# Raw query and key weights in tiles of their own, and a fixed order of two engines in the last two products

## The chip, the cores and the metric

The kernel runs on one core of a Trainium2 chip. The metric is the device time of one execution in microseconds (us), the median of several runs. The core has five engines with a queue each: PE (TensorE, matmuls; its weight loads are shown apart as PEld), DVE (VectorE), ACT (ScalarE), POOL (GpSimd) and SP (SyncE), which here issues nearly all DMAs. Each engine takes its own queue in order; semaphores tie them together.

## The reference, cut to what matters

One layer of an encoder for 1024 frames of 1024 channels, in float32:

```
h = x + W_out( GroupRMSNorm( concat[ attention(n), conv(n), gating(n) ] ) ),   n = RMSNorm(x) * g
y = RMSNorm( h + W_down( relu( W_up RMSNorm(h) )^2 ) ) * g_final

attention: 8 heads of 64; queries of a chunk of 64 frames see their own chunk and the 8 before it,
           scores * 64**-0.5 + bias by clipped distance, softmax, times values
```

The query, key and value columns are part of one input projection `w_in` (512 columns each). The last step is an RMSNorm: each row of 1024 is divided by the root of its mean square and multiplied by a gain.

## The kernel before, in words

All products are made in a split form: a float32 operand is written as a rounded part `hi` (ACT, a copy, L52) and a remainder `lo` (DVE, a subtraction, L53), and one product is three matmuls (`mm3`, L64 to L66). So each weight that comes in raw by DMA costs one ACT and one DVE instruction (`split`) before PE can use it.

**Attention.** Heads go in four pairs p = 0 to 3. For each pair the key weights (a raw tile of 128 x 1024) and the query weights are loaded (`Proj.load`, L344), split into the slots `wh` and `wl` of pool `W` (two each), and multiplied with the normed input in two halves of 512 frames (`Proj.steps`); `evac` (L388) copies each half from PSUM into the projected rows `kc` or `qc`. `expand` (L398 to L403) then makes from `kc` and `qc` the operands of each of the two heads: `kh`, `kl` and `q`, with two copies by DMA (L399, L401). The raw weights and the projected rows have one and the same tile: `raw` takes a tile of tag `QC` (two slots, one for keys and one for queries), the load writes the weights into it, the split reads them, and the evacuation writes the rows over them. So the raw key weights of pair p + 1 need the slot in which the projected keys of pair p lie, until the last `expand` of pair p has read it.

The 64 units of attention (pair, head, tile of 128 frames) run in a loop: `softmax` of the next unit, `turn` (transposes of the probabilities to `pt` on PE, split into `pth` on ACT, L510, and `ptl` on DVE, L511), `values` (L537) and `scores`. Between them `fill_to` feeds PE with steps of the projections of the later pairs and of the other two branches, in the order of `stream`: keys and queries of pair 1, `cg` 0, keys and queries of pair 2, `xh` 0, keys and queries of pair 3, and so on. `expand` for the first head of pair p + 1 stands at unit 12 of pair p, for the second at unit 15. `stream` splits the next weights in the middle of a projection and issues the load of the ones after.

**The order of the work.** Outside of blocks of `manual_schedule` a planner orders each engine's queue: by the order of the program, but with an estimate of when operands and slots are there, so an instruction that it holds ready goes ahead of one that waits. In a block of `manual_schedule` the engines that are named take their instructions in the order of the program.

**The end.** The down projection is seven products per block of the inner dimension (`PLAN`), four blocks. The last two products of the last block (m = 3 and m = 4) each finish four tiles of 128 rows, one PSUM bank after another: bank u of 4 takes 12 matmuls, then `add` puts it on the accumulator `acc` (DVE, L876). `finish` follows: `square` of the half that was just added (ACT, L1166, with the sum over the row), the sum of both halves scaled (DVE, L1176), the power -1/2 (POOL, L1178), the two halves scaled into `o` (DVE, L1184; for the last tile one half on ACT, L1182) and two writes (SP, L1185). The tile `o` has two buffers.

Of the kernel before, what the change touches and what calls it, by code (L numbers as in the profile page):

```python
# [30 lines left out]
def trunk(ctx, tc, x, mix_g, w_in, rb_rev, conv_w, sg_ln_g, sg_ln_b, sg_w, sg_b,  # L31
# [13 lines left out]
    def big(tag, shape, dt, name):  # L45
        return L.tile(shape, dt, tag=tag, bufs=SLOTS[tag], name=name)
# [52 lines left out]
    def half(hf):  # L99
        return slice(hf * HALF, (hf + 1) * HALF)  # L100
# [280 lines left out]
    def qk_projs(p):  # L381
        def one(nm, c0, sc):
            def raw():
                qkc[nm, p] = big("QC", [P, T], F32, f"{nm}c{p}")
                return qkc[nm, p].rearrange("p (k m) -> p k m", k=NK)

            def evac(hf, ps):
                A.activation(qkc[nm, p][:, hf * HALF:(hf + 1) * HALF], ps, AF.Copy, scale=sc)  # L388
            return Proj(c0 + p * P, f"{nm}{p}", evac, raw)
        return [(o, hf) for o in (one("k", 512, 1.0), one("q", 0, 0.125)) for hf in range(2)]  # L390
# [484 lines left out]
    def add(out, a, b):  # L875
        V.tensor_tensor(out, a, b, op=ALU.add)  # L876
# [291 lines left out]
    def early_half(t, k):  # L1168
        square(t, k)
        V.tensor_scalar(sums[t][:, 2:3], sums[t][:, k:k + 1], 1.0 / D, EPS, op0=ALU.mult, op1=ALU.add)  # L1170

    def finish(t, k):

        ss = sums.get(t)
        square(t, k)
        V.scalar_tensor_tensor(ss[:, 3:4], ss[:, k:k + 1], 1.0 / D, ss[:, 2:3], op0=ALU.mult, op1=ALU.add)  # L1176
        r = sm.tile([P, 1], F32, tag="rf", name="rf")
        G.tensor_tensor(r, ss[:, 3:4], mhalf[:, 0:1], op=ALU.pow)  # L1178
        o = E_.tile([P, D], F32, tag="o", bufs=2, name=f"o{t}")
        for i in (k, 1 - k):  # L1180
            if t + 1 == NT and i != k:
                A.activation(o[:, half(i)], acc[t][:, half(i)], AF.Copy, scale=r)  # L1182
            else:
                V.scalar_tensor_tensor(o[:, half(i)], acc[t][:, half(i)], r, gfin[:, half(i)], op0=ALU.mult, op1=ALU.mult)  # L1184
            load(out[t * P:(t + 1) * P, half(i)], o[:, half(i)])  # L1185
# [11 lines left out]
        ready[n] = [down_ops(PLAN[s][0], p) for p in BLOCKS[b]]  # L1197

    load_down(BLOCKS[0], (1,))
    banks = {}  # L1200
    for n, (b, s) in enumerate(steps):
        if n + 1 < len(steps):
            prep(n + 1)
        if n == 0:
            open_acc(0, 0)
            load_down(BLOCKS[0], (0,))
        elif n in (2, 3, 5):
            open_acc(*{2: (0, 1), 3: (1, 1), 5: (1, 0)}[n])
        elif n == 14:
            load(gfin, fin_g.partition_broadcast(P))  # L1210
        m, which, start, (i, k) = PLAN[s]
        ops = ready.pop(n)
        last = b == len(BLOCKS) - 1
        for u in range(4):
            sl = slice(u * P, (u + 1) * P)
            if start:
                banks[which, u] = bank(f"d{which}{u}")
            ps = banks[which, u]
            for j, (ho, wo_) in enumerate(ops):
                mm3(ps, ho[:, 0, sl], ho[:, 1, sl], wo_[:, 0], wo_[:, 1], start and j == 0, j == len(ops) - 1,  # L1220
                    skip_group_check=True)
            t = 4 * i + u
            add(acc[t][:, half(k)], ps, acc[t][:, half(k)])
            if last and m in (2, 7):
                early_half(t, k)
            if last and m == 7 and t + 1 == NT:
                V.tensor_tensor(acc[t][:, half(k)], acc[t][:, half(k)], gfin[:, half(k)], op=ALU.mult)
            if last and m in (3, 4):
                finish(t, k)


_INS = ["x", "mix_norm_g", "w_in", "rel_bias", "conv_w", "sg_ln_g", "sg_ln_b", "sg_w", "sg_b",
# [24 lines left out]
```

## Time and profile before

| | |
|---|---|
| median of 3 runs | 1120.9 us (1120.43 to 1121.08) |
| the profiled execution, its own time | 1118.65 us |
| span of the profiled execution (first to last instruction) | 1116.9 us |
| PE busy | 1090.4 us (98%) |
| weight loads busy | 911.8 us (82%) |
| DVE, ACT, POOL busy | 746.9 (67%), 551.5 (49%), 73.2 us (7%) |

The page of the profile gives busy times for one execution; the span is shorter than the execution's own time by what lies before the first and after the last instruction. In the page's slices of 28 us PE is busy at nine tenths or more in all but the first and the last. Views of the trace used below: the waits (who waited for whom, in total us, times, and the longest), the timeline (start, duration, engine, line, operation, and in brackets the idle time before it with what ended it), the instructions of one tile, windows (busy us of each engine in a stretch) and the DMA issues.

### The profile page before, as it was taken

What the parts mean: (1) busy time and instruction counts of PE and PEld (TensorE: products, weight loads), DVE (VectorE), ACT (ScalarE), POOL (GpSimd) and SP (SyncE); (2) the same over time, 40 slices, a digit from 0 to 9 for tenths busy, and PEclk for the clock granted to TensorE, in tenths of its full rate; (3) what the DMA queues carried; (4) which work ended last, traced back from release to release, by engine and by line L of the source; (5) the groups of instructions that cost most, each with busy time, mean ns of one, the idle gap of its engine ahead of it and who ended that gap; (6) DMA issues with size and microseconds to landing.
All of it is one profiled execution on the core that took longest, in us unless ns stands there. A gap on an engine that the chain in (4) does not pass through costs nothing.

```text
span 1116.9 us, 14983 instructions
## 1 busy us (share of the span) xinstructions
PE 1090.4 (98%) x5377; PEld 911.8 (82%) x5377; DVE 746.9 (67%) x1430; ACT 551.5 (49%) x1094; POOL 73.2 (7%) x131
## 2 busy tenths in 40 slices
PE   7999999999999999999999999999999999999996
PEld 6889987887888788887888888888878888888884
DVE  5526477667676761569766656564499978869775
ACT  5434376555664630467555555555544433434442
POOL 1101023101021210000000000000000000000001
PEclk8999999999999999999999999999999999999998
DMA  7523013021120143452543535353698545263303
GB/s 244 184 68 80 1 24 88 18 53 47 43 58 23 39 151 131 151 208 104 177 172 122 189 115 196 113 189 125 250 340 280 196 165 188 86 207 103 96 20 150
DMA packets 83197, 145.16 MB, mean 130 GB/s; under 512 B 6050, under 2 KB 41652, under 8 KB 83124
## 3 DMA queue, kind: packets, MB, share of 16 engines
q1 hardware_dynamic: 82548, 142.38, 37.8%
q10 hardware_dynamic: 576, 1.84, 0.4%
q8 instruction: 42, 0.69, 0.3%
q14 instruction: 31, 0.25, 0.1%
HBM read 98.58 MB, written 41.42 MB: 125 GB/s over the span
## 4 chain that ended last, share of the span: by engine, by line
PE 85%; DVE 7%; DMA 4%; ACT 2%; issue 1%; POOL 0%; SPq 0%; POOLq 0%; DVEq 0%; ACTq 0%
PE uA L66 5%; PE uA L65 5%; PE uA L64 5%; PE dA L66 5%; PE dA L64 5%; PE dA L65 4%; PE dB L64 3%; PE dB L66 3%; PE dB L65 3%; PE av L537 3%; PE uC L64 2%; PE uC L66 2%; PE uC L65 2%; PE o L64 2%; PE o L65 2%; PE o L66 2%
## 5 line engine op out<-in xcount | busy, mean ns | idle before, releaser
L52 ACT ACTIVATE ho<-hr 128x512 fp32r<-128x512 f32 x112 | 69.0, 623 | 140.7 <-PE dA L66 51.2
L64 PE MATMUL dA<-wo,ho 128*128 128x512 f32 x256 | 99.7, 390 | 0.8 <-ACT ho L52 0.8
L66 PE MATMUL dA<-wo,ho 128*128 128x512 f32 x256 | 99.3, 390 | 0.5 <-DVE ho L53 0.5
L65 PE MATMUL dA<-wo,ho 128*128 128x512 f32 x256 | 99.5, 389 | 0.0
L53 DVE TENSOR_TENSOR ho<-hr,ho 128x512 fp32r<-128x512 f32 x112 | 76.8, 690 | 15.7 <-ACT ho L52 15.7
L64 PE MATMUL dB<-wo,ho 128*128 128x512 f32 x192 | 74.8, 390 | 0.0
L66 PE MATMUL dB<-wo,ho 128*128 128x512 f32 x192 | 74.8, 390 | 0.0
L65 PE MATMUL dB<-wo,ho 128*128 128x512 f32 x192 | 74.7, 389 | 0.0
L53 DVE TENSOR_TENSOR wo<-wd,wo 128x512 fp32r<-128x512 f32 x96 | 65.6, 689 | 2.3 <-ACT wo L52 2.3
L52 ACT ACTIVATE wo<-wd 128x512 fp32r<-128x512 f32 x96 | 58.8, 619 | 10.1 <-DVE wd L879 6.2
L485 ACT ACTIVATE pr<-s,st 128x640 f32<-128x640 f32 (+2 forms) x64 | 42.3, 661 | 36.9 <-DVE st L480 26.6
L64 PEld LDWEIGHTS dA<-wo,ho 128*128 128x128 f32 x256 | 48.0, 188 | 11.3 <-ACT ho L52 1.5
L66 PEld LDWEIGHTS dA<-wo,ho 128*128 128x128 f32 x256 | 48.0, 188 | 11.1 <-DVE ho L53 1.1
L65 PEld LDWEIGHTS dA<-wo,ho 128*128 128x128 f32 x256 | 48.1, 188 | 9.9
L510 ACT ACTIVATE pth<-pt 128x512 fp32r<-128x512 f32 (+2 forms) x96 | 40.0, 435 | 32.1 <-PE pt L506 31.4
L876 DVE TENSOR_TENSOR acc<-dA,acc 128x512 f32<-128x512 f32 x64 | 43.8, 690 | 16.7 <-PE dA L66 15.0
L511 DVE TENSOR_TENSOR ptl<-pt,pth 128x512 fp32r<-128x512 f32 (+2 forms) x96 | 45.2, 487 | 12.9 <-ACT pth L510 11.9
L64 PE MATMUL o<-woh,mxh 128*128 128x512 f32 x128 | 50.6, 399 | 0.0
L66 PE MATMUL o<-woh,mxl 128*128 128x512 f32 x128 | 50.0, 391 | 0.0
L65 PE MATMUL o<-wol,mxh 128*128 128x512 f32 x128 | 50.0, 390 | 0.0
L1178 POOL TENSOR_TENSOR rf<-ssf,mhalf 128x1 f32<-128x1 f32 x8 | 4.4, 551 | 617.4 <-DVE ssf L1176 617.4
L876 DVE TENSOR_TENSOR hid<-uC,v 128x512 f32<-128x512 f32 x15 | 10.4, 691 | 51.5 <-PE uC L66 51.5
(344 smaller groups left out, 3083.0 us busy)
## 6 DMA issues: line engine op xcount, KB each, us to landing
wr_u<-in_w_up SPq DMA_DIRECT2D x32, 512.0 KB, 4.3
wd<-in_w_down SPq DMA_DIRECT2D x32, 512.0 KB, 4.6
wr_o<-in_w_out SPq DMA_DIRECT2D x8, 512.0 KB, 4.3
xr<-in_x SPq DMA_DIRECT2D x8, 512.0 KB, 4.9
hs<-h SPq DMA_DIRECT2D x8, 512.0 KB, 3.7
acc<-hs SPq DMA_DIRECT2D x16, 256.0 KB, 6.5
out_y<-o SPq DMA_DIRECT2D x16, 256.0 KB, 2.1
x<-in_x SPq DMA_DIRECT2D x7, 512.0 KB, 3.9
```

The costliest lines, as they stand in the source:

```text
L52: A.activation(hi, raw, AF.Copy)
L53: V.tensor_tensor(lo, raw, hi.bitcast(F32), op=ALU.subtract)
L64: PE.matmul(ps, lhsT=sh, rhs=mh, start=start, stop=False, **kw)
L65: PE.matmul(ps, lhsT=sh, rhs=ml, start=False, stop=False, **kw)
L66: PE.matmul(ps, lhsT=sl, rhs=mh, start=False, stop=stop, **kw)
L485: A.activation(pr[:, :b - a], s[:, a:b], AF.Exp, bias=st[:, 2:3], accum_out=lsum[p, t // 4][:, lc:lc + 1])
L510: A.activation(dh, src, AF.Copy)
L511: V.tensor_tensor(dl, src, dh.bitcast(F32), op=ALU.subtract)
L537: PE.matmul(dst, lhsT=lhs, rhs=rhs, start=first, stop=(i == len(kbs) - 1 and ph == 1))
L876: V.tensor_tensor(out, a, b, op=ALU.add)
L1178: G.tensor_tensor(r, ss[:, 3:4], mhalf[:, 0:1], op=ALU.pow)
```

## The change

First, the raw weights of keys and queries get a tag of their own, `kw`, in the pool of the attention stage, with two slots; the tile of tag `QC` is taken at the first evacuation, for the projected rows alone. Second, from the last product but one on, ACT and DVE are in a block of `manual_schedule`, and `finish` is taken apart: `square` follows the add of its tile at once, `rate` (sum and power) comes ahead of the next tile's add, and the scalings and writes of a tile come after the add and the square of the next.

```diff
--- before.py
+++ after.py
@@ -381,10 +381,11 @@
     def qk_projs(p):
         def one(nm, c0, sc):
             def raw():
-                qkc[nm, p] = big("QC", [P, T], F32, f"{nm}c{p}")
-                return qkc[nm, p].rearrange("p (k m) -> p k m", k=NK)
+                return AP_.tile([P, NK, P], F32, tag="kw", bufs=2, name=f"wr_{nm}{p}")
 
             def evac(hf, ps):
+                if hf == 0:
+                    qkc[nm, p] = big("QC", [P, T], F32, f"{nm}c{p}")
                 A.activation(qkc[nm, p][:, hf * HALF:(hf + 1) * HALF], ps, AF.Copy, scale=sc)
             return Proj(c0 + p * P, f"{nm}{p}", evac, raw)
         return [(o, hf) for o in (one("k", 512, 1.0), one("q", 0, 0.125)) for hf in range(2)]
@@ -1169,13 +1170,15 @@
         square(t, k)
         V.tensor_scalar(sums[t][:, 2:3], sums[t][:, k:k + 1], 1.0 / D, EPS, op0=ALU.mult, op1=ALU.add)
 
+    def rate(t, k):
+
+        ss = sums[t]
+        V.scalar_tensor_tensor(ss[:, 3:4], ss[:, k:k + 1], 1.0 / D, ss[:, 2:3], op0=ALU.mult, op1=ALU.add)
+        rates[t] = sm.tile([P, 1], F32, tag="rf", name="rf")
+        G.tensor_tensor(rates[t], ss[:, 3:4], mhalf[:, 0:1], op=ALU.pow)
+
     def finish(t, k):
-
-        ss = sums.get(t)
-        square(t, k)
-        V.scalar_tensor_tensor(ss[:, 3:4], ss[:, k:k + 1], 1.0 / D, ss[:, 2:3], op0=ALU.mult, op1=ALU.add)
-        r = sm.tile([P, 1], F32, tag="rf", name="rf")
-        G.tensor_tensor(r, ss[:, 3:4], mhalf[:, 0:1], op=ALU.pow)
+        r = rates[t]
         o = E_.tile([P, D], F32, tag="o", bufs=2, name=f"o{t}")
         for i in (k, 1 - k):
             if t + 1 == NT and i != k:
@@ -1197,7 +1200,7 @@
         ready[n] = [down_ops(PLAN[s][0], p) for p in BLOCKS[b]]
 
     load_down(BLOCKS[0], (1,))
-    banks = {}
+    banks, whole, rates, man = {}, [], {}, ExitStack()
     for n, (b, s) in enumerate(steps):
         if n + 1 < len(steps):
             prep(n + 1)
@@ -1211,6 +1214,8 @@
         m, which, start, (i, k) = PLAN[s]
         ops = ready.pop(n)
         last = b == len(BLOCKS) - 1
+        if n + 2 == len(steps):
+            man.enter_context(tc.manual_schedule(engines={mybir.EngineType.Activation, mybir.EngineType.DVE}))
         for u in range(4):
             sl = slice(u * P, (u + 1) * P)
             if start:
@@ -1220,13 +1225,21 @@
                 mm3(ps, ho[:, 0, sl], ho[:, 1, sl], wo_[:, 0], wo_[:, 1], start and j == 0, j == len(ops) - 1,
                     skip_group_check=True)
             t = 4 * i + u
+            if whole:
+                rate(*whole[0])
             add(acc[t][:, half(k)], ps, acc[t][:, half(k)])
             if last and m in (2, 7):
                 early_half(t, k)
             if last and m == 7 and t + 1 == NT:
                 V.tensor_tensor(acc[t][:, half(k)], acc[t][:, half(k)], gfin[:, half(k)], op=ALU.mult)
             if last and m in (3, 4):
-                finish(t, k)
+                square(t, k)
+                whole.append((t, k))
+                if len(whole) > 1:
+                    finish(*whole.pop(0))
+    rate(*whole[0])
+    finish(*whole.pop())
+    man.close()
 
 
 _INS = ["x", "mix_norm_g", "w_in", "rel_bias", "conv_w", "sg_ln_g", "sg_ln_b", "sg_w", "sg_b",
```

## Rows read from the trace of the kernel before

**Rows 1.** The page, its first line.
```profile
span 1116.9 us, 14983 instructions
```

**Rows 2.** Waits of PE, then of its weight loads: total us, times, longest.
```profile
PE pt L506 <- DVE ptl L511: 3.7, 2, 1.9
...
PEld pt L506 <- DVE ptl L511: 4.5, 2, 2.3
```

**Rows 3.** Timeline around 190 us: start, us, engine, line, operation [idle before, releaser].
```profile
185.04 1.22 DVE L400 TENSOR_TENSOR kl<-kc,kh 64x1024 fp32r<-64x1024 f32 x1
186.29 0.39 SPq L344 DMA_DIRECT2D kc<-in_w_in  x1
...
192.22 1.06 ACT L52 ACTIVATE wh_k<-kc 128x1024 fp32r<-128x1024 f32 x1 [1.91 <-DMA kc<-in_w_in]
192.34 0.34 PE L466 MATMUL s<-kh,q 128*128 128x384 f32 x1
192.52 0.33 PE L467 MATMUL s<-kl,q 128*128 128x384 f32 x1
...
193.32 1.22 DVE L53 TENSOR_TENSOR wl_k<-kc,wh_k 128x1024 fp32r<-128x1024 f32 x1 [2.22 <-ACT wh_k L52]
194.46 0.28 DVE L511 TENSOR_TENSOR ptl<-pt,pth 128x128 fp32r<-128x128 f32 x1
194.80 0.33 PE L506 MATMUL pt<-ident,pr 128*128 128x128 f32 x1 [1.94 <-DVE ptl L511]
```

**Rows 4.** Timeline around 250 us.
```profile
256.18 0.40 PE L65 MATMUL xh<-nl,wh_xh 128*128 128x512 f32 x1
...
258.37 0.33 PE L506 MATMUL pt<-ident,pr 128*128 128x128 f32 x1 [1.80 <-DVE ptl L511]
```

**Rows 5.** Timeline of PE, its last 48 matmuls, first and last.
```profile
1095.07 0.39 PE L64 MATMUL dA<-wo,ho 128*128 128x512 f32 x1
...
1105.72 0.39 PE L66 MATMUL dA<-wo,ho 128*128 128x512 f32 x1
```

**Rows 6.** Timeline of DVE at the end, from the last add but one.
```profile
1107.83 0.68 DVE L876 TENSOR_TENSOR acc<-dA,acc 128x512 f32<-128x512 f32 x1
1109.37 0.16 DVE L1176 SCALAR_TENSOR_TENSOR ssf<-ssf 128x1 f32<-128x1 f32 x1 [0.85 <-ACT sq L1166]
1109.44 0.69 DVE L876 TENSOR_TENSOR acc<-dA,acc 128x512 f32<-128x512 f32 x1
1110.19 1.42 DVE L1184 SCALAR_TENSOR_TENSOR o<-acc,rf,gfin 128x512 f32<-128x512 f32 x2
1111.52 0.15 DVE L1176 SCALAR_TENSOR_TENSOR ssf<-ssf 128x1 f32<-128x1 f32 x1
1112.34 0.75 DVE L1184 SCALAR_TENSOR_TENSOR o<-acc,rf,gfin 128x512 f32<-128x512 f32 x1 [0.66 <-POOL rf L1178]
```

**Rows 7.** Timelines of SP (97 to 158 us) and ACT (175 us).
```profile
97.23 0.56 SPq L344 DMA_DIRECT2D qc<-in_w_in  x1
157.94 0.47 SPq L399 DMA_DIRECT2D kh<-kh  x1
...
175.74 0.60 ACT L388 ACTIVATE qc<-q 128x512 f32<-128x512 f32 x1 [0.57 <-PE q L66]
```

**Rows 8.** Tiles `xn` and `xT`: durations, first and last start.
```profile
L91 DVE SCALAR_TENSOR_TENSOR xn<-x,rs,gmix x7: 1277/1284/1285, 16.0 to 35.8; 128x1024 f32<-128x1024 f32 x7
...
L218 PE MATMUL xT<-ident,xn x64: 270/273/476, 9.9 to 54.5; 128*128 128x128 f32 x64
```

**Rows 9.** Timelines of ACT and POOL at the end.
```profile
1108.61 0.63 ACT L1166 ACTIVATE sq<-acc 128x512 f32<-128x512 f32 x1 [2.97 <-DVE acc L876]
...
1109.61 0.55 POOL L1178 TENSOR_TENSOR rf<-ssf,mhalf 128x1 f32<-128x1 f32 x1 [3.14 <-DVE ssf L1176]
```

**Rows 10.** DMA issues of the output: size, us to landing.
```profile
out_y<-o SPq DMA_DIRECT2D x16, 256.0 KB, 2.1
```

**Rows 11.** Windows: stretch, length, busy PE, PEld, DVE, ACT, POOL, clock, DMA.
```profile
380.00:390.00 10.00, 7.63 (x50) 6.41 (x49) 7.94 (x15) 9.27 (x17) 2.65 (x3) 0.94 0.16 57
```

## The prediction

> **What bounds the kernel now.** I read the page first, then the waits of TensorE (PE), then the timeline at the places which they name, then the chain of work that ended last. The page gives a span of 1116.9 us [rows 1]; PE is the engine that is nearly always busy in it, so a gain is either a hole in PE's row that closes or a tail after PE's last matmul that gets shorter. The waits of PE and of its weight loads have one entry of size in the middle of the kernel: the transposes `pt` wait for DVE's `ptl`, two times, 3.7 us in the matmul row and 4.5 us in the weight load row [rows 2]. Both lie in the attention stage, at 192.5 and 256.4 us, and the timeline shows one and the same chain [rows 3, 4]. The reader is to see how a DMA that is late by one step becomes a hole in PE two engines further on: DVE's `kl` (L400) reads the old projected key `kc`; 1.25 us after its start, when it is through, SP issues the load of the next key weights into that same slot (186.29); it lands 5.9 us later, when ACT's `wh_k` starts (192.22); DVE has `wl_k` next in its order and waits 2.22 us for ACT; the small `ptl` that PE needs stands behind `wl_k` (194.46), and PE idles until 194.80. The chain of work that ended last leaves PE at its end: the last matmul starts at 1105.72 and takes 0.39, so PE is done at 1106.11 [rows 5], but DVE adds that bank only at 1109.44 [rows 6], and the span runs 10.8 us beyond PE.
>
> **Part 1, raw weights in tiles of their own.** Removed: the tie of eight loads (four keys, four queries) to the release of the projected rows. Added: two slots; no instruction, and the same eight loads and splits. Moved: a load can go out once the split two loads earlier is done; the projected rows take their slot when they are evacuated instead. The key weights of head pair 2 could then be loaded after the split of pair 1, around 100 us, and there the SP queue issues nothing between 97.23 and 157.94 [rows 7], so they are in place long before 186. What the split still needs is a weight slot, and that is free when the last matmul of the query of pair 1 has read it, right before its evacuation at 175.74 [rows 7]. So `wh_k` can run at about 176 to 190 instead of 192.2, and `wl_k` no longer stands waiting in front of `ptl`. In the same way the key of pair 3 moves up, and with it the second hole goes.
>
> What a closed hole is worth: matmuls are pipelined, so I count from start to start. The matmul ahead of the first hole starts at 192.52 with 384 columns; its twin, equal in form, started 0.18 us before it, at 192.34. Without the wait `pt` would have started at 192.70; it started at 194.80: 2.10 us [rows 3]. Ahead of the second hole a 512-column matmul starts at 256.18; of the last 48 matmuls of that form, at the end of the kernel, the first and the last start 10.65 us apart [rows 5], so 0.227 from one to the next; `pt` could have started at 256.41 and did at 258.37: 1.96 us [rows 4]. Sum 4.06 us. It lies between the two bounds that the waits give, 3.7 and 4.5 [rows 2]. PE has more work queued behind each hole, so it shows one to one in the span.
>
> The Trainium skill, "Trainium Kernel Development and Optimization", section "Performance Expectations", holds matmul busy time a bad metric, because matmuls are pipelined, and the LDWEIGHTS busy share a good one. By that row part 1 would be worth 4.5 us and the sum below would be 8.0 instead of 7.5. The trace speaks for a value between, since the start of a weight load runs ahead of its matmul.
>
> Below, the bound of part 1 is not zero but a loss: a planner orders the queues by its own estimate of times, and with loads ready at other times it may order the whole attention stage otherwise. Each split is 1.06 us of ACT and 1.22 of DVE [rows 3], and wherever it is put ahead of work that PE waits for it can cost a hole like the two here. The early loads themselves I cost at nothing: the first that moves far is the key of pair 1, which may go out from about 22 us on, beside the loads of `x`. Their cover is the norm of the last `x` tile, which starts at 35.8 and takes 1.3 while the last transpose that reads it starts at 54.5 [rows 8]: 17 us of slack, against 5.9 us for a load [rows 3]. SP takes its queue in order, so a load that waits for its slot holds up the copies of `kh` and `kl` behind it; two such waits (at 186.29 and its like for pair 3) go, and the new ones wait for splits, at times when the queue is thin.
>
> **Part 2, the order at the end.** Nothing is added or removed: eight sums, eight powers, eight pairs of scalings stay. What moves: before, DVE's order put both scalings of a tile ahead of the next tile's add, and waited for the power in between. One tile went 1107.83 add, 1108.61 square on ACT, 1109.37 sum, 1109.61 power on POOL, 1110.19 scaling [rows 6, 9]: steps of 0.78, 0.76, 0.24 and 0.58 us. Now tile t's scalings stand behind the add of t+1. DVE's work for a tile is 0.08 (sum: 1109.37 to 1109.44), 0.60 (an add's 0.69 overlaps the next by some 0.09) and 1.33 (scaling, 1110.19 to 1111.52) [rows 6], 2.0 us together; PE needs 12 times 0.227 = 2.72 for it. So DVE keeps up, and each add starts when PE ends its bank.
>
> The last tile then: PE ends at 1106.11; add at 1106.14; the scalings of tile 6, whose power has long been there, 1106.74 to 1108.07; the square was ready for the sum at 1106.14 + 0.78 + 0.76 = 1107.68, so the sum goes at 1108.07; power 1108.31; last scalings 1108.89. Before they began at 1112.34 [rows 6]. Gain 3.45 us. What follows them (scaling, write, end of the program: 1112.34 to 1116.9, 4.56 us) stays. What is late next is the scalings of tile 6 ahead of the last sum, 0.39 us. New wait: the add of t+1 stands in front of tile t's scalings, which wait up to 0.7 us for PE; nobody waits for these but the writes. An output tile is used again two tiles later: its second half is written about 4.1 us before (2 x 2.72 - 1.33), and a write lands in 2.1 [rows 10]. Bounds: 0 (the writes cannot follow) to 3.84 (tile 6's scalings out of the way as well).
>
> **Sum.** 4.06 + 3.45 = 7.5 us off. Against the profiled execution, 1118.65 us with its span of 1116.9 and 1.75 around it, this gives 1111.1. The runs of before have their median at 1120.9, 2.25 above that execution; taken from there, 1113.4.
>
> **The rivals.**
> First, **only the end gains**: the loads are still issued late, or in the attention stage another wait of PE for `ptl` takes the place of the two. For it: DVE is a single queue and PE waits for what stands in it. Against it: among PE's waits `pt` has `ptl` with a count of two [rows 2], so at all the other tiles of the stage the same queue lets PE through without an entry of that kind. 1120.9 - 3.45 = 1117.4.
> Second, **only the keys gain**, since writes or DVE hold the end as before: 1120.9 - 4.06 = 1116.8. Against it is the 0.7 us of room in each of DVE's rounds.
> Third, **more than forecast**: the end of the attention stage has a hole too, PE busy 7.63 of 10 us [rows 11]; it lies in the same order of queues, and if it goes by luck as well: 2.37 more, 1111.0. Nothing in the change aims there.
> Fourth, **slower**: the planner, which believes that the loads are in place, puts splits early into ACT's and DVE's queues, and they stand there until PE lets go of a weight slot, with `ptl` behind them. The place is the attention stage, the price 2.03 us each (the mean of the two holes). Six splits can move (keys and queries of pairs 1 to 3). Six such holes cost 12.2, less the 4.06 of today and 3.45 at the end: 4.7 us slower, 1125.6. It decides from the fourth on (8.1 against 7.5), and can be told from no change from the fifth. Against it: a slot is free at 175.74, and the planner has 16 us to place a split.
> Fifth, **nothing**: each gain is given back elsewhere, 1120.9.
>
> **How the numbers follow.** Both gains 0.60, the end alone 0.14, the keys alone 0.07, more 0.06, nothing 0.06, slower 0.07. Faster by over 0.2% (2.2 us, about what a measurement of this kernel can tell from no change) are the first four: 0.87; same 0.06; slower 0.07. The likeliest is 1113.4. The range goes from the third rival, 1111.0, down a little for the bound of 4.5, to 1110.6; upwards past the two halves (1116.8 and 1117.4) to 1118.0 for a half that falls short. It leaves out 0.13.
>
> **What would show it.** Key loads for pairs 2 and 3 issued long before the two holes; no wait of `pt` for `ptl` of 1.8 us; a PE busy time of 10 of 10 around 190 to 200 and 250 to 260. At the end eight adds spaced 2.7 us, the last within 0.1 us of PE's last matmul, and 7.3 us from PE's end to the span's. I am wrong if PE shows new holes between 100 and 390, if the splits of the keys wait for PE in ACT's queue, or if DVE's scalings wait for a write.

## The result and the profile after

The changed kernel takes 1113.42 us in the median of five runs (1109.73 to 1115.3); the kernel before, beside it, 1120.43. The ratio is 0.9941 with a 95% interval of 0.9923 to 0.9958: 6.6 us faster, 4.7 to 8.6. The ratios here and below leave out three single executions that took far longer than all others of their kernel (1209.22 us in e1, 5708.38 in e3, 1359.99 in e6). The profiled execution of after took 1109.73 us, the shortest of the five and 8.9 less than that of before (1118.65). The page of after, its first line and its line of busy times:

```profile
span 1108.0 us, 14987 instructions
PE 1089.7 (98%) x5377; PEld 909.7 (82%) x5377; DVE 746.8 (67%) x1430; ACT 552.3 (50%) x1094; POOL 72.3 (7%) x131
```

The busy times are those of before to within a few us, so what went is mostly idle time, of PE or behind its last matmul. Line numbers of after are one higher than those of before from L386 on, three higher in the scalings of the last norm (L1184 is L1187).

**The holes.** Answering to [rows 2], the longest waits of PE in after (total us, times, longest):

```profile
PE xT L218 <- DVE xn L231: 3.7, 1, 3.7
PE warm L245 <- DVE wz L242: 1.1, 1, 1.1
PE Ra L432 <- DVE ptl L512: 1.1, 1, 1.1
PE pt L507 <- DVE ya L541: 1.1, 2, 0.9
```

The entry `pt` for `ptl` (3.7 us over two) is gone, and PE is busy for 9.83 and 9.97 us in the stretches 190 to 200 and 250 to 260, where it was busy for 8.06 and 8.20 before. The loads of the raw key weights (duration in ns, first and last start), and the timeline of after around the split of pair 2, which answers to [rows 3]:

```profile
L344 SPq DMA_DIRECT2D wr_k<-in_w_in x3: 373/377/378, 22.1 to 178.6; - x3
```

```profile
135.73 0.37 SPq L344 DMA_DIRECT2D wr_k<-in_w_in  x1
...
175.62 1.06 ACT L52 ACTIVATE wh_k<-wr_k 128x1024 fp32r<-128x1024 f32 x1
...
177.34 1.22 DVE L53 TENSOR_TENSOR wl_k<-wr_k,wh_k 128x1024 fp32r<-128x1024 f32 x1
```

The load that went out at 186.29 now goes at 135.73. `wh_k` stands at 175.62 instead of 192.22, with no idle time in brackets: ACT didn't wait for a DMA ahead of it. `wl_k` follows at 177.34, 0.66 us after `wh_k` is done, and DVE doesn't wait ahead of it either.

**The tail.** PE's last matmul, and DVE from the last add but one; they answer to [rows 5, 6]:

```profile
1100.25 0.39 PE L66 MATMUL dA<-wo,ho 128*128 128x512 f32 x1
```

```profile
1097.96 0.69 DVE L877 TENSOR_TENSOR acc<-dA,acc 128x512 f32<-128x512 f32 x1 [0.64 <-PE dA L66]
1098.57 1.40 DVE L1187 SCALAR_TENSOR_TENSOR o<-acc,rf,gfin 128x512 f32<-128x512 f32 x2
1099.89 0.15 DVE L1176 SCALAR_TENSOR_TENSOR ssf<-ssf 128x1 f32<-128x1 f32 x1
1100.68 0.69 DVE L877 TENSOR_TENSOR acc<-dA,acc 128x512 f32<-128x512 f32 x1 [0.64 <-PE dA L66]
1101.29 1.41 DVE L1187 SCALAR_TENSOR_TENSOR o<-acc,rf,gfin 128x512 f32<-128x512 f32 x2
1102.61 0.15 DVE L1176 SCALAR_TENSOR_TENSOR ssf<-ssf 128x1 f32<-128x1 f32 x1
1103.42 0.75 DVE L1187 SCALAR_TENSOR_TENSOR o<-acc,rf,gfin 128x512 f32<-128x512 f32 x1 [0.66 <-POOL rf L1178]
```

The last adds lie 2.72 us apart and each now waits for PE (0.64), where before PE was long through. The last add starts 0.04 us after PE's end (1100.64), and the span ends 7.36 us after it instead of 10.79.

**Where the 8.9 us lie.** To set stages side by side I cut each span at the starts of five matmuls that every version has: the one to `colsT` (the end of the start-up), the last to `bg` in line 66 (in the late part of attention), the last to `o`, the last to the tile `uA` of the up projection with `t40h` (1.4 us ahead of the last to `uA`), these also in L66, and the last one of all; the tail counts from PE's end, 0.39 us later. Lengths in us, rounded, so differences can be 0.1 off; e1b to e12 are the experiments below, and the last two columns give the granted clock in the windows 384 to 390 and 390 to 396 us (1.00 is the full clock, 0.50 the lower of its two levels; a value between is a window with both):

| | start | attention | to `o` | up | down | tail | span | clock | clock |
|---|---|---|---|---|---|---|---|---|---|
| before | 65.7 | 315.6 | 105.8 | 310.9 | 307.8 | 10.8 | 1116.9 | .90 | .82 |
| after | 66.1 | 312.5 | 104.2 | 310.3 | 307.2 | 7.4 | 1108.0 | 1.00 | 1.00 |
| e11 (after once more) | 67.1 | 312.5 | 107.3 | 310.7 | 307.3 | 7.4 | 1112.8 | .70 | .73 |
| e1b (part 1 alone) | 67.2 | 312.5 | 104.2 | 313.1 | 306.8 | 10.8 | 1115.0 | 1.00 | 1.00 |
| e2 (part 2 alone) | 67.0 | 317.0 | 104.3 | 311.2 | 306.7 | 7.4 | 1113.9 | 1.00 | 1.00 |
| e3 (a third slot) | 65.8 | 312.5 | 105.7 | 311.3 | 307.6 | 10.8 | 1114.2 | .73 | .98 |
| e4 (split later in program) | 66.8 | 316.2 | 105.8 | 310.4 | 306.4 | 10.8 | 1116.8 | 1.00 | .72 |
| e10 (split behind `ptl`) | 67.1 | 311.2 | 105.8 | 311.7 | 307.4 | 10.8 | 1114.3 | .72 | 1.00 |
| e5 (no fixed order) | 67.7 | 312.5 | 107.3 | 311.3 | 307.7 | 11.8 | 1118.8 | .79 | .64 |
| e6 (old sequence, fixed) | 67.1 | 312.4 | 105.7 | 311.0 | 307.2 | 13.8 | 1117.5 | .82 | .89 |
| e8 (last sum earlier) | 65.5 | 312.4 | 105.7 | 310.7 | 306.6 | 7.4 | 1108.8 | .72 | 1.00 |
| e7 (one slot) | 65.9 | 312.4 | 104.2 | 310.5 | 309.8 | 7.4 | 1110.6 | 1.00 | 1.00 |
| e12 (e10 and part 2) | 65.5 | 311.2 | 107.3 | 310.8 | 307.0 | 7.4 | 1109.5 | .50 | .95 |

After against before: attention -3.1, tail -3.4, the stretch behind attention -1.6, the up and down stages -0.6 each, the start +0.4. The first two are what the change aims at. The third is a stretch in which the two kernels have the same code, and the windows of before (first two lines) and of after show what differs (length, busy us with counts of PE, PEld, DVE, ACT, POOL, then granted clock, DMA share, GB/s):

```profile
384.00:390.00 6.00, 4.01 (x27) 3.52 (x27) 5.69 (x10) 5.89 (x11) 0.41 (x1) 0.90 0.25 87
390.00:396.00 6.00, 6.00 (x28) 5.24 (x28) 4.73 (x6) 3.55 (x7) 2.76 (x2) 0.82 0.40 132
```

```profile
384.00:390.00 6.00, 5.05 (x34) 4.69 (x35) 5.72 (x10) 5.12 (x9) 3.29 (x2) 1.00 0.34 126
390.00:396.00 6.00, 6.00 (x28) 4.95 (x27) 3.04 (x5) 3.04 (x5) 0.20 (x1) 1.00 0.80 266
```

In both PE has idle time at the end of attention; in before the clock granted in these 12 us fell to the lower level for a part of them, in after it did not. Whether that belongs to the change is asked by e2, e1b and e11.

### The profile page after: what moved, and what is told of

Its sections match the earlier page's. It is cut to its first block, busy times and chain, and to the rows that moved or that the text cites. A ratio compares the mean times of both kernels' runs of the same rounds, so it can differ in the third digit from the quotient of the medians.

```text
span 1108.0 us, 14987 instructions
## 1 busy us (share of the span) xinstructions
PE 1089.7 (98%) x5377; PEld 909.7 (82%) x5377; DVE 746.8 (67%) x1430; ACT 552.3 (50%) x1094; POOL 72.3 (7%) x131
## 4 chain that ended last, share of the span: by engine, by line
PE 88%; DVE 5%; DMA 3%; ACT 1%; issue 1%; SPq 0%; POOL 0%; POOLq 0%; DVEq 0%; ACTq 0%
PE dA L66 5%; PE dA L64 5%; PE dA L65 5%; PE uA L66 5%; PE uA L65 5%; PE uA L64 5%; PE dB L66 4%; PE dB L64 4%; PE dB L65 4%; PE av L538 3%; PE uC L64 2%; PE uC L66 2%; PE uC L65 2%; PE pt L507 2%; PE o L64 2%; PE o L66 2%
## 5 line engine op out<-in xcount | busy, mean ns | idle before, releaser
L66 PE MATMUL dA<-wo,ho 128*128 128x512 f32 x256 | 99.3, 390 | 0.5 <-DVE ho L53 0.5
L66 PE MATMUL dB<-wo,ho 128*128 128x512 f32 x192 | 74.9, 390 | 0.0
L52 ACT ACTIVATE wo<-wd 128x512 fp32r<-128x512 f32 x96 | 58.6, 618 | 10.8 <-DVE wd L880 6.8
L66 PEld LDWEIGHTS dA<-wo,ho 128*128 128x128 f32 x256 | 48.0, 188 | 11.0 <-DVE ho L53 1.1
L66 PE MATMUL o<-woh,mxl 128*128 128x512 f32 x128 | 50.0, 391 | 0.0
```

Of the source, the lines that this page charges most:

```text
L52: A.activation(hi, raw, AF.Copy)
L66: PE.matmul(ps, lhsT=sl, rhs=mh, start=False, stop=stop, **kw)
```

## The experiments

The theory: a late load, tied to the old projected rows, puts `wl_k` into DVE's queue ahead of `ptl` while it waits, which is the holes' whole cause; and the order of DVE makes the longer tail. The rivals are in each expectation.

### e1_tiles and e1b_tiles: the first part alone

```diff
-                square(t, k)
-                whole.append((t, k))
-                if len(whole) > 1:
-                    finish(*whole.pop(0))
+                finish(t, k)
```

The rest of `finish` and the block of `manual_schedule` go back as in before.

> The kernel before with part 1 alone (raw query and key weights in tiles of their own), the end as before. Theory (two holes of PE at the key splits close, 4.06 us, the end is worth 3.45 by itself): 4.1 us under before, between 3 and 5.5, since PE of the changed kernel ended 5.5 us earlier; PE waits for ptl no longer for 1.8 us or more. Rival (the attention stage gained by a new order of the planner, not by the holes): the holes close but PE's end moves by something else than the 4 us. Rival (part 1 worth nothing by itself): within 1 us of before. The tail from PE's end to the span's end stays at 10.8 us in all cases.

Ratio 0.9972 (0.9957 to 0.9987): -3.1 us, -1.5 to -4.8. The same kernel was run once more for a trace.

> Part 1 alone once more, for a profile at the full clock. Theory: attention stage 3.1 to 3.2 us shorter than before, PE's waits as in the changed kernel, the tail from PE's last matmul to the span's end 10.8 us as before. Rival: the tail differs from before by more than 0.5 us, so that part 1 has a share in it.

1116.72 us in that one run, attention 312.5, tail 10.8, and the stretch behind attention 104.2 at full clock. The first part brings 3.0 us by the trace's attention stage (315.56 less 312.53 before rounding); 4.06 had been expected. The span is only 1.9 us shorter than that of before, since this one execution had a longer start-up (67.2) and a longer up stage (313.1), in which the granted clock fell to 0.72 in the window 516 to 522, where PE waits 1.9 us for DVE's `a1l`.

### e2_order: the second part alone

```diff
-                return AP_.tile([P, NK, P], F32, tag="kw", bufs=2, name=f"wr_{nm}{p}")
+                qkc[nm, p] = big("QC", [P, T], F32, f"{nm}c{p}")
+                return qkc[nm, p].rearrange("p (k m) -> p k m", k=NK)
 
             def evac(hf, ps):
-                if hf == 0:
-                    qkc[nm, p] = big("QC", [P, T], F32, f"{nm}c{p}")
```

> The kernel before with part 2 alone (fixed order of DVE and ACT in the last two products, scalings behind the next add); the raw weights stay in the tiles of the projected rows. Theory: 3.4 us under before, PE's last matmul ends at 1106 us as before and the span 7.4 us after it; the two holes at 192.5 and 256.4 us stay. Rival (the tail gains only with the earlier PE): under 1 us.

Ratio 0.9972 (0.9956 to 0.9988): -3.1 us, -1.3 to -4.9. The tail is 7.4 us, as in after, and the holes stay. PE's longest wait in attention, and two windows behind the second hole:

```profile
PE pt L506 <- DVE ptl L511: 4.0, 2, 2.0
```

```profile
256.00:262.00 6.00, 3.95 (x18) 3.10 (x17) 3.28 (x8) 1.96 (x5) 0.00 (x0) 0.81 0.39 83
262.00:268.00 6.00, 6.00 (x37) 5.39 (x37) 3.33 (x8) 3.51 (x7) 1.59 (x3) 0.90 0.01 3
```

The parts add up: 0.9972 times 0.9972 is 0.9944, and the changed kernel has 0.9941. A side result: this kernel has the attention code of before, holes included, and yet the stretch behind attention took 104.3 us at full clock, as in after. So the 1.6 us there are no gain of the first part. On the other hand the clock fell to 0.81 and 0.90 behind the second hole here, which it did not in the profile of before, and attention took 317.0 us.

### e3_qc3: the tie stays, with a third slot

```diff
-    SLOTS = {"N": 16, "QK": 6, "QC": 2, "VY": 10}
+    SLOTS = {"N": 16, "QK": 6, "QC": 3, "VY": 10}
```

This is before, end included: raw weights and projected rows still share a tile.

> The kernel before with three slots instead of two for the tag of the projected query and key rows; the raw weights still share tiles with the rows, the end as before. Theory (what counts is that the key load waits for the release of a slot): the spare slot lets the key weights of pairs 2 and 3 load early, both holes of PE close, about 4 us under before, as part 1 alone; the query loads still wait. Rival (the sharing of a tile by weights and rows is what costs, in the order that the planner makes of it): the holes stay, within 1 us of before.

Ratio 0.9962 (0.9948 to 0.9976): -4.3 us, -2.7 to -5.8. The holes are gone, with the weights still in the tiles of the rows, and attention is 312.5, as with tiles of their own. The waits of PE and of its weight loads in it:

```profile
PE pt L506 <- DVE ya L540: 1.1, 2, 0.9
PE av L537 <- DVE ptl L511: 0.7, 3, 0.2
```

```profile
PEld av L537 <- DVE ptl L511: 3.5, 7, 0.7
PEld pt L506 <- DVE ya L540: 3.3, 9, 0.6
```

So it was the wait for a slot. The tag of the tile matters only through the number of slots.

### e7_kw1: one slot for the raw weights

```diff
-                return AP_.tile([P, NK, P], F32, tag="kw", bufs=2, name=f"wr_{nm}{p}")
+                return AP_.tile([P, NK, P], F32, tag="kw", bufs=1, name=f"wr_{nm}{p}")
```

> The changed kernel with one slot instead of two for the raw weights. Theory (a load is needed only some 8 us ahead of its split, and one slot lets the key weights of pair 2 go out once the query of pair 1 is split, about 140 us, against a split at 176): no hole comes back, the time is the changed kernel's within 1.5 us. Rival (the depth of two is what takes the load off the path): PE waits for ptl 1.5 us or more again at one or two places, 2 to 4 us over the changed kernel.

Ratio 0.9956 (0.9942 to 0.9971), attention 312.4, no hole: in attention one slot does. In the down stage this one profile has a wait of PE that the others lack, `dB` for `ho`, 2.0 us, where ACT waits 5.92 us for the load of `hr`; behind it the clock falls to 0.76 in the window 808 to 814, and the stage takes 309.8 us. Why that load came late was not followed up.

### e4_late_split and e10_behind: the load as late as before, the split elsewhere

The question of these two: is it the late weights that cost, or only the place at which their split stands in DVE's queue? First, the split of the key weights of pairs 2 and 3 is called eight steps later in the program:

```diff
-                    if nx < len(order) and order[nx] not in ready:
+                    late = nx < len(order) and order[nx].name in ("k2", "k3") and hf == 0
+                    if not late and nx < len(order) and order[nx] not in ready:
                         order[nx].split()
```

> The kernel before, but the split of the key weights of pairs 2 and 3 stands 8 steps later in the program (in the second half of the projection before it), with the loads where the slot lets them be. Theory (the hole comes from DVE standing at the split, with ptl queued behind it, not from PE lacking weights): the splits come later than ptl, PE's two waits of 1.8 to 1.9 us for ptl shrink to under 0.5 us, 3 to 4 us under before although the loads are as late as before. Rival (the key weights themselves come too late for PE): the holes stay or move to PE waiting for wl_k, no gain, or slower by up to 3 us.

Ratio 0.9989 (0.997 to 1.0008), nothing that can be told from no change. The timeline says why:

```profile
193.23 1.06 ACT L52 ACTIVATE wh_k<-kc 128x1024 fp32r<-128x1024 f32 x1 [1.86 <-DMA kc<-in_w_in]
194.33 1.23 DVE L53 TENSOR_TENSOR wl_k<-kc,wh_k 128x1024 fp32r<-128x1024 f32 x1 [2.17 <-ACT wh_k L52]
195.47 0.28 DVE L512 TENSOR_TENSOR ptl<-pt,pth 128x128 fp32r<-128x128 f32 x1
195.81 0.33 PE L507 MATMUL pt<-ident,pr 128*128 128x128 f32 x1 [1.89 <-DVE ptl L512]
```

The planner still put the split ahead of `ptl`: the queue's order had not changed, so this run tested nothing but that a later place in the program is not a later place in the queue. Its two waits are 1.9 and 1.0 us, and behind the first the clock fell (0.72 in the window 196 to 202), which shows in its attention stage of 316.2 us: the first matmul to `xh` starts 174.5 us after `colsT`, in before 173.0. The next kernel fixes the place of both instructions of the split, `wh_k` on ACT and `wl_k` on DVE, in their queues, on top of e4's edit:

```diff
-            split(self.r, self.hi, self.lo)
+            if self.name in ("k2", "k3"):
+                with tc.issue_after(last_turn["A"]), tc.issue_after(last_turn["V"]):
+                    split(self.r, self.hi, self.lo)
...
-            A.activation(dh, src, AF.Copy)
-            V.tensor_tensor(dl, src, dh.bitcast(F32), op=ALU.subtract)
+            last_turn["A"] = A.activation(dh, src, AF.Copy).ins
+            last_turn["V"] = V.tensor_tensor(dl, src, dh.bitcast(F32), op=ALU.subtract).ins
```

> The kernel before, with the split of the key weights of pairs 2 and 3 at the later place in the program (as e4) and queued, on ACT and on DVE, behind the split of the probabilities of the unit traced before it; the loads are as late as before, two slots, the end as before. Theory (the hole is DVE standing at the weights' split ahead of ptl): the load still goes out at about 187 us, but ptl no longer stands behind wl_k, the two waits of PE for ptl (1.8 to 1.9 us) go, PE's end comes 3 to 4 us earlier. Rival (PE lacks the key weights): the wait comes back as PE or its weight loads waiting for wh_k or wl_k, within 1 us of before.

Ratio 0.9944 (0.9928 to 0.9961): -6.3 us, -4.4 to -8.1, with the end as before. Its timeline at the first hole, and the waits of its weight loads from 100 to 375 us:

```profile
187.70 0.39 SPq L344 DMA_DIRECT2D kc<-in_w_in  x1
...
193.37 0.28 ACT L515 ACTIVATE pth<-pt 128x128 fp32r<-128x128 f32 x1
193.54 1.05 ACT L52 ACTIVATE wh_k<-kc 128x1024 fp32r<-128x1024 f32 x1
193.92 0.28 DVE L516 TENSOR_TENSOR ptl<-pt,pth 128x128 fp32r<-128x128 f32 x1
194.62 1.23 DVE L53 TENSOR_TENSOR wl_k<-kc,wh_k 128x1024 fp32r<-128x1024 f32 x1 [0.42 <-ACT wh_k L52]
```

```profile
PEld av L542 <- DVE ptl L516: 2.8, 6, 0.7
PEld pt L511 <- DVE ya L545: 1.8, 6, 0.5
```

The load goes as late as in before (187.70), `wh_k` comes as late, and PE has no hole: `pth` is ahead of `wh_k`, and `ptl` is through before `wl_k`. Late weights alone cost nothing; the parked instructions ahead of ready work did. And attention is 311.2 us here, 1.3 shorter than in the changed kernel.

The order of ACT has a part in this that the prediction leaves out. `ptl` needs `pth`, and in before ACT has `pth` behind `wh_k`, for which it sits idle 1.91 and 2.06 us until the load is there, at both holes:

```profile
193.19 0.26 ACT L510 ACTIVATE pth<-pt 128x128 fp32r<-128x128 f32 x1
...
256.76 0.26 ACT L510 ACTIVATE pth<-pt 128x128 fp32r<-128x128 f32 x1
```

`pth` is done at 193.45 and 257.02, and `ptl` starts at 194.46 and 258.03. So with DVE's order alone put right, `ptl` could have come 1.01 us earlier at each hole, about half of the 2 us, and with ACT's alone `ptl` would still have stood behind `wl_k`. This is an estimate from these rows: e10 moves both engines' instructions, and no run moves one alone.

### e5_no_fix: the steps taken apart, without the fixed order

The line that enters `manual_schedule` is left out, all else as in after.

```diff
-            man.enter_context(tc.manual_schedule(engines={mybir.EngineType.Activation, mybir.EngineType.DVE}))
+            pass
```

> The changed kernel without the block of fixed order; sums, powers and scalings stand in the program as in the changed kernel. Theory (the planner puts a scaling that is ready ahead of an add that still waits for PE, and the fixed order is what forbids it): DVE has each tile's two scalings ahead of the next add again, the tail from PE's last matmul to the span's end is 10 to 11 us instead of 7.4, 3 us over the changed kernel. Rival (the order of the text is enough): tail 7.4 us.

Ratio 0.9989 (0.9974 to 1.0004). DVE at the end:

```profile
1107.50 0.75 DVE L1187 SCALAR_TENSOR_TENSOR o<-acc,rf,gfin 128x512 f32<-128x512 f32 x1 [0.66 <-POOL rf L1178]
1108.17 0.68 DVE L877 TENSOR_TENSOR acc<-dA,acc 128x512 f32<-128x512 f32 x1
...
1111.85 0.68 DVE L877 TENSOR_TENSOR acc<-dA,acc 128x512 f32<-128x512 f32 x1
```

The planner puts scalings that wait for the power (0.66) ahead of adds that are ready, and the last two adds fall to 3.68 us apart. The tail is 11.8 us, longer than the 10.8 of before.

### e6_fix_old: the fixed order, with the old sequence

```diff
-            if whole:
-                rate(*whole[0])
...
-                if len(whole) > 1:
-                    finish(*whole.pop(0))
-    rate(*whole[0])
-    finish(*whole.pop())
+                rate(*whole[0])
+                finish(*whole.pop(0))
```

> The changed kernel with the fixed order, but the steps of a tile not taken apart: add, square, sum, power and both scalings of a tile, then the next tile's add. Theory (what counts is that nothing waits for POOL in front of an add): DVE needs 3.69 us for a tile (1107.83 less 1104.14 in the trace of before) against PE's 2.72, last add 7 x 3.69 = 25.8 us after the first, the tail 13.9 us: 6.5 us over the changed kernel, 2 to 3 over before less what the attention stage gives. Rival (the fixed order itself gains): tail under 10 us.

Ratio 1.0007 (0.9992 to 1.0022): a tail of 13.8 us and adds 3.69 us apart (1106.93 and 1110.62), which takes back what the first part had gained. Neither half of the second part is worth anything alone: the sequence must be right, and it must be held.

### e8_last: the last sum between the two scalings of tile 6

The 0.39 us that the prediction named as late next: the last tile's sum waits for both scalings of tile 6. `finish` takes one argument more, which says which of the two halves it scales (not shown).

```diff
...
-                    finish(*whole.pop(0))
+                    finish(*whole[0], (0,) if t + 1 == NT else (0, 1))
+                    done_ = whole.pop(0)
     rate(*whole[0])
+    finish(*done_, (1,))
     finish(*whole.pop())
```

> The changed kernel with the sum and the power of the last tile between the two scalings of the tile before it, instead of behind both. Theory (the scalings of tile 6 are what is late in front of the last sum, 0.39 us): the tail from PE's end to the span's end 7.0 us instead of 7.4; the time is the changed kernel's within its noise. Rival (the last sum waits for the square anyway, or the write of tile 6 becomes late): tail 7.3 us or more.

Ratio 0.9931 (0.9906 to 0.9956), not to be told from the changed kernel, and the tail is 7.4 us. DVE and POOL at the end:

```profile
1102.03 0.74 DVE L1191 SCALAR_TENSOR_TENSOR o<-acc,rf,gfin 128x512 f32<-128x512 f32 x1
1102.96 0.16 DVE L1176 SCALAR_TENSOR_TENSOR ssf<-ssf 128x1 f32<-128x1 f32 x1 [0.19 <-ACT sq L1167]
1103.04 0.74 DVE L1191 SCALAR_TENSOR_TENSOR o<-acc,rf,gfin 128x512 f32<-128x512 f32 x1
1104.22 0.75 DVE L1191 SCALAR_TENSOR_TENSOR o<-acc,rf,gfin 128x512 f32<-128x512 f32 x1 [0.44 <-POOL rf L1178]
```

```profile
1100.86 0.55 POOL L1178 TENSOR_TENSOR rf<-ssf,mhalf 128x1 f32<-128x1 f32 x1 [2.17 <-DVE ssf L1176]
1103.20 0.99 POOL L1178 TENSOR_TENSOR rf<-ssf,mhalf 128x1 f32<-128x1 f32 x1 [1.79 <-DVE ssf L1176]
```

The sum did come earlier (1.58 us after PE's end at 1101.38, against 1.97 in after), and the power behind it took 0.99 us instead of 0.55: it ran beside a scaling. What was won was lost again there.

### e11_after: the changed kernel once more

> The changed kernel itself once more, beside the three others on one chip. In its first profile the attention stage (from the transpose of the gains to the last bg matmul) was 3.2 us shorter than before, the stretch behind it to the last o matmul 1.6 us shorter with the granted clock at 1.00 throughout where before had 0.82 to 0.90. Theory (those 1.6 us belong to the execution, not to the change): over many runs 3.2 + 3.45 = 6.6 us under before (0.9941), and this profile may show the dip of the clock at 384 to 396 us again. Rival (the change cures the dip): 8 us or more under before, no dip.

Ratio 0.9944 (0.9926 to 0.9961), 1114.11 us. Its attention and tail are those of after to 0.1 us, and the windows at the end of attention are these:

```profile
384.00:390.00 6.00, 4.26 (x18) 3.81 (x19) 4.99 (x10) 4.94 (x8) 1.34 (x1) 0.70 0.25 87
390.00:396.00 6.00, 6.00 (x27) 5.29 (x26) 4.17 (x6) 2.90 (x5) 1.83 (x2) 0.73 0.53 176
```

The same kernel, with the clock at 0.70 and 0.73: the stretch behind attention takes 107.3 us, 3.1 more than in the profile of after and 1.6 more than in that of before. So its length belongs to the single execution, and not to the change.

### e12_both: e10's queue and the second part

e10's edits on the changed kernel, with the raw weights back in the tiles of the rows (as e2's diff has it), so without the two added slots.

> The queueing of e10 (key splits of pairs 2 and 3 behind the probabilities' split, raw weights still in the tiles of the projected rows, loads as late as before) together with the fixed order at the end. Theory (part 1 gains by the order of DVE's queue alone, and the two parts add): attention stage 4.4 us shorter as in e10, tail 3.4 us shorter, 7.8 us under before, so 0 to 2 us under the changed kernel, without the two added tiles. Rival (the early loads are worth something by themselves): 1 us or more over the changed kernel.

Ratio 0.9919 (0.9902 to 0.9937), 1111.45 us, the fastest of the kernels whose ratio was taken. Attention 311.2 as in e10, tail 7.4 as in after. The windows 180 to 200 us, of after and then of e12:

```profile
180.00:200.00 20.00, 19.60 (x121) 16.18 (x120) 14.18 (x39) 12.41 (x27) 3.39 (x9) 1.00 0.43 110
```

```profile
180.00:200.00 20.00, 19.94 (x122) 17.08 (x121) 15.33 (x41) 13.56 (x30) 5.15 (x10) 1.00 0.58 139
```

In the matmul row (second number) the two look alike; in the weight loads (third) e12 has 0.90 us more work done. The median lies 2.7 us under e11's, in the same comparison with before; the traces show 1.3 of it, in attention, and the intervals of the two ratios overlap.

## Why the prediction was right, and where it was not

**The sum and the number.** Forecast were 7.5 us off and 1113.4 us; measured were 6.6 by the ratio (4.7 to 8.6) and 1113.42. The terms as the traces have them are 3.1 (attention) and 3.4 (tail), together 6.5. That the number agrees so closely has a part of chance in it: the kernel before ran 0.5 us faster beside the changed one than in the runs from which I started. The profiled execution of after is 8.9 us shorter, and 1.6 of that is the clock behind attention, which e2, e1b and e11 show not to be the change.

**Part 1, the mechanism.** Right as far as it goes, and shown: e3 closes the holes by a slot alone, e10 by the order of ACT's and DVE's queues alone, with the load as late as before. What it left out is ACT: the prediction's chain has `ptl` behind `wl_k` on DVE, but `pth`, which `ptl` needs, also stood behind `wh_k` on ACT, so that, by the estimate given with e10, DVE's order alone makes about half of each hole. An earlier load cures both, so the forecast didn't suffer by it. `wh_k` came at 175.62, at the early end of the 176 to 190 that I gave. The load of pair 2 went out at 135.73, not around 100; that was still 40 us ahead of its split, so it cost nothing. The cover that I named for the early load of pair 1 held: it goes at 22.1, and the start-up is 66.1 us against 65.7, inside the 65.5 to 67.7 of the other versions.

**Part 1, the size.** Mis-sized: 4.06 us forecast, 3.0 to 3.2 measured in eight profiles without the holes (312.4 to 312.5 against 315.6). The two holes went whole, so the term counted what was taken away rightly; what failed is the sentence that it shows one to one in the span since PE has more work queued behind each hole. Two matmuls that all versions have, the first to `xh` (behind the first hole) and the first to `bg` (behind both), show where. In us from the start of `colsT`:

| | `xh` | `bg` | first hole brings | second brings |
|---|---|---|---|---|
| before | 173.03 | 259.16 | | |
| after | 171.93 | 256.13 | 1.10 | 1.93 |
| e10 | 171.03 | 254.82 | 2.00 | 2.34 |

In e10, where the splits stand behind the work that PE waits for, the holes bring 4.34 us, a little over the 4.06 (2.10 and 1.96). In after, 0.90 of that is lost at the first and 0.41 at the second. The moved split is DVE work that stands in a queue again, 1.22 us ahead of other things that PE needs. The weight loads show it. In the span 100 to 375 us of after they wait:

```profile
PEld av L538 <- DVE ptl L512: 3.5, 7, 0.6
PEld pt L507 <- DVE ya L541: 3.3, 9, 0.6
```

and in the same stretch of before:

```profile
PEld av L537 <- DVE ptl L511: 2.7, 6, 0.7
PEld pt L506 <- DVE ya L540: 1.6, 5, 0.5
```

2.5 us of small waits were added, 16 in place of 11, none over 0.6 us long. In e10 and e12 these two lines read nearly as in before (2.8 over 6, 1.8 over 6). For the first split the sizes meet: between 174 and 200 us, right behind the moved `wl_k` (177.34), after has

```profile
PEld pt L507 <- DVE ya L541: 1.0, 2, 0.6
```

and e10 has no such wait in its same stretch (175 to 201), where it gains the 0.90 us. So the slower rival of the prediction, splits that stand ahead of `ptl`, did come, at a small size: not parked, since no split waits long for a slot, but in the way, at 0.9 and 0.4 us for the two that moved instead of the 2.03 that I priced. That the added waits are what is missing is still an inference from these rows and from e10; the order of DVE between the two differs in more than one place, and no run changes one of them alone.

I took bounds of 3.7 and 4.5 from the waits of the matmuls and of the weight loads. The measured 3.1 lies under both: such bounds hold for what goes, not for what comes. Taking the weight loads' row as the price would have put the term at 4.5 and so further off; yet in the search for the small waits it was the better row, since for these two the matmul row of after shows 0.9 us in that stretch (0.7 and 0.2) where the weight loads show 6.8. The Trainium skill, "Trainium Kernel Development and Optimization", section "Performance Expectations", calls the busy share of weight loads a good metric, and matmul busy time a bad one, for how close a kernel is to its roofline; it doesn't say that a single hole is priced so, and here that price missed.

**Part 2.** Right, step by step. Tail 7.36 for 7.3; adds 2.72 us apart for 2.7; last add 0.04 us behind PE for under 0.1; the last scalings 2.78 us after PE's end (1103.42 less 1100.64) for 2.78 (1108.89 less 1106.11). Gain 3.43 in the profile for 3.45, and e2 alone gives 3.1 (1.3 to 4.9). No scaling waited for a write. One reading was too general: that both scalings of a tile stood ahead of the next tile's add. At the very end [rows 6] have the last add (1109.44) ahead of tile 6's scalings (1110.19) and right behind its sum (1109.37), which waited for the square; the sum of the steps is not touched by it. The sum's delay of 0.39 us behind the scalings of tile 6 was named rightly, but my upper bound of 3.84 took it to be free for the asking; e8 shows that it is not, as the power then runs beside a scaling and takes 0.99 us instead of 0.55.

**The rivals.** Only the end or only the keys gaining: both halves gain, each alone 3.1. More than forecast, with the hole at the end of attention gone: the idle time is still there (PE is busy 9.6 of the 12 us from 378 to 390 in before, after and e11 alike), and it is the clock behind it that comes and goes. Nothing: excluded by the interval.

**Still open.** Why e10 and e12 gain 6.3 and 9.1 us by their ratios where their traces show 4.4 and 7.8: both lie inside the intervals (4.4 to 8.1, and 7.1 to 11.0). If the clock falls behind the holes in some executions of before, as in e2 and e4, the mean price of a hole is above that of before's profile; but then the changed kernel should gain that too, and its ratio doesn't show it.

## What to carry to other kernels

A hole in a saturated engine is traced back until an instruction is found that waits at the head of another engine's queue with ready work behind it, and further back along that work's own inputs, since the same wait can sit in a second queue (here ACT's, with `pth`); then the cheapest cure is to move the waiting instructions behind the ready work (e10, no memory, 311.2 us), and the second cheapest to have their input earlier (e3, e7 and the change, 312.4 to 312.5). An operation moved out of a hole still lands somewhere: here the small waits that it made there showed among the weight loads and hardly among the matmuls. To defer an epilogue by one tile needs both the deferred sequence and an order that is enforced; either alone was nothing or worse (tails of 11.8 and 13.8 us against 7.4 with both and 10.8 with neither).

## What the runs showed of the hardware

**The clock after a pause of PE is not the same in each execution.** At the end of attention PE is busy 9.6 of the 12 us from 378 to 390 in before, after, e1b, e7, e8, e10 and e11. Yet the granted clock in the windows from 384 to 396 was 1.00 in after, e1b, e7 and also e2, and fell to between 0.50 and 0.90 in one or both windows of the nine others, and the stretch behind attention took 104.2 to 104.3, 105.7 to 105.8 or 107.3 us. This is about 1.6 or 3.1 us that two profiles can differ by with no cause in the code. It can follow a pause elsewhere as well: a hole within attention in e2 (317.0 us against 315.6 in before, where the holes are the same) and in e4, and single waits of PE in the up stage of e1b (0.72) and the down stage of e7 (0.76). What decides it, the runs don't show.

**A tiny POOL instruction beside a DVE instruction, seen once.** The power on 128 values took 0.55 us in all eight places of after, and 0.99 us in e8 where it ran beside a scaling whose two tensor inputs, `acc` and `gfin`, both lie in SBUF. It ended at 1104.19, 0.41 us after that scaling. The Trainium skill, "SBUF — State Buffer", section "Who interferes with whom", has this rule: a DVE instruction with two SBUF inputs and a GpSimd instruction that reads SBUF contend for a shared pair of ports, and the order of issue decides which of them is held up. e8's two rows agree with it (scaling at 1103.04, power at 1103.20); no run takes the scaling's second SBUF input away to test it. An add, one of whose inputs comes from PSUM, did no harm beside a power: in before one at 1099.91 on DVE (0.69 us) overlaps the power at 1100.08, which took 0.55.
